# Hybrid SSM, pooling and attention layer: SSM groups every 7.5 steps, their memory handed to the output stage during the last projections, output weights requested earlier

## The chip, the cores and the metric

One core of a Trainium2 chip runs the whole layer in one launch. The metric is the device time of an execution in microseconds. The kernel before took 1631.17 us in the median of three runs (1629.35 to 1631.57).

## The reference

The input x has 4096 tokens of 1024 channels in fp32. One layer is computed:

```
h = RMSNorm_pre(x)
su, sg, pu, pg, q, k, v, ag = split(h @ w_in)            # widths 256 256 256 256 512 128 128 512
y_ssm  = GLU(GELU(S5(su) + D*su)) * silu(sg)             # 16 groups, 64 complex states, both directions
y_pool = scale * GroupLinear(mean pools(pu) - pu) * silu(pg)
y_attn = windowed attention(q, k, v) * silu(ag)          # +-128 tokens, 8 heads, 2 KV heads
out = x + RMSNorm_post(concat(y_ssm, y_pool, y_attn) @ w_out)
```

## The kernel before

The tokens are cut into NB = 8 blocks of 512 (TB), a block into four tiles of 128. The channels are cut into NK = 8 chunks of 128. Each product in the large matrices is made of three matmuls on operands split into a high and a low part (hi·hi, hi·lo, lo·hi), so that weights and activations are split by ScalarE (a copy, L173) and VectorE (a subtraction, L162), function `split`.

The order of the work is written out by hand. `Slots` (L84) holds a table from step number to actions. `e.at(n, f)` puts f into step n, `e.gen` runs a generator whose `yield n` is a pause of n steps, and `e.step()` emits the actions of the present step, in the order in which they were put there. The main loop emits six matmuls of 512 columns and then calls `e.step()`: a step is six matmuls of TensorE's order. Each engine, and SyncE, which issues nearly all DMAs, runs its instructions in the order in which they were emitted and waits for semaphores in that order.

The stages, by steps: projections of the first kind (0 to 191), query, key and value projections (192 to 383) with attention behind them, gate projections (384 to 575, `p3_block`: six chunks of four steps in each of eight blocks), and from 576 on the output stage (`w_out_k`: one step for one token tile and one chunk, eight steps for a tile).

Step 422 (48·NB + ATT_TAIL) calls `to_p3`. It opens the pools of the SSM stage and plans the 16 SSM groups, group g from step 422 + int(8·g) on, the last one at 542. A group's actions (list at L1080) are numbered from its start: load 0, angles 3 (GpSimd), their sines 5 to 7 (ScalarE), input products 9, direct product 10, `turn_re` 10 and `turn_im` 11 (VectorE, with a GpSimd sum in 11), `turn_sum` 12 (GpSimd), scans 13 and 14, `back_cos` 16 (VectorE), `back_sin` 17 and `back_sum` 20 and 21 (GpSimd), state products 24 and 25 (TensorE), copy 26, store 28. The SSM products are in fp32 and run as two instructions each. The tile wt of a group has two buffers.

The last gate block begins at step b0 = 552. In it each chunk n ends at step 552 + 4n + 3; one step later ScalarE evacuates its PSUM bank (two banks in turn, L1122), and three steps after that SyncE stores the gate (L1123). After each of these chunks `load_wo` asks for the two halves of output weight chunk 2 + n (256 KB each, three buffers "raw") and splits them four steps later, the subtraction another step later. The weights take the buffers that the projection weights of the chunk have released.

The first mixer tiles: pooling of block 0 (`y_pool`, two rounds of GpSimd sums, a ScalarE copy and VectorE operations) from step 546, attention tiles (`y_attn`) from 563 and 570. In the output stage 18 steps use chunks 2 to 7 of three token tiles. At the seventh of them, step 582, `to_c` finishes what is left of gates and SSM, closes the pools "gp" and "sv" of the SSM stage, opens the last stage's pools in their memory, and starts `y_ssm(0)` (its GLU products eight steps later), the loads of weight chunks 0 and 1, two residual tiles and the mixer tiles of block 1. The loop that follows (L1429) waits, by empty steps, until `YK[0, 0]` and `YK[0, 1]` of `y_ssm(0)` are there.

Of the kernel before, what the change touches and what calls it, by code (L numbers as in the profile page):

```python
# [10 lines left out]
F32 = mybir.dt.float32  # L11
F32R = mybir.dt.float32r
# [4 lines left out]
P = 128  # L17
SEQ = 4096
DM = 1024
# [53 lines left out]
    return c  # L73


SSM_PACE = 8.0
ATT_TAIL = 38
WARM = 8
P2_OPEN = 24 * NB + 15
# [50 lines left out]
def hybrid_kernel(ctx, tc, A, out):  # L130
# [56 lines left out]
    def split(hi, lo, src, eng, lag=1, scale=None):  # L187

        copy(hi, src)
        if lag:  # L190
            e.at(e.now + lag, lo_part, lo, src, hi, eng)
        else:
            lo_part(lo, src, hi, eng)
# [99 lines left out]
    def sched_x(b):  # L293
        b0 = 24 * b
        if b >= NB + RAWB:
            for i, d in enumerate((-12, -10, -4, -3)):
                e.at(b0 + d, x_load, b, i, label="main")
            return
        for i, (d, n_, sp_) in enumerate(((-22, -14, -13), (-20, -12, -11), (-18, -10, -4), (-16, -8, -3))):
            e.at(b0 + d, x_dma, b, i, label="main")  # L300
            if b == 1:
                e.at(b0 - 15 + 2 * i, x_sq, b, i, label="main")
                n_, sp_ = (-2, -2, -2, -1)[i], (-2, -2, -1, 0)[i]
            e.at(b0 + n_, x_norm, b, i, label="main")
            e.at(b0 + sp_, x_split, b, i, label="main")
# [648 lines left out]
    def p3_open():  # L954
        cw = ctx.enter_context(tc.tile_pool(name="cw", bufs=1))
        XTP[0] = ctx.enter_context(tc.tile_pool(name="xt3", bufs=3))
        ph = ExitStack()
        gp = ph.enter_context(tc.tile_pool(name="gp", bufs=3))
        sv = ph.enter_context(tc.tile_pool(name="sv", bufs=1))
        GP[0] = (gp, "g", "p3")  # L960
        rho = cw.tile([P, G], F32, name="rho")
        dma(out=rho, in_=rhod[:, :])
        psc = cw.tile([P, 2], F32, name="psc")
        dma(out=psc, in_=A["pool_scale"])
        gbc = cw.tile([P, DM], F32, name="gbc")
        dma(out=gbc, in_=A["post_g"])
        glb = cw.tile([P, 6], F32, name="glb")
        dma(out=glb[:, 0:4], in_=A["glu_b"])
        ts(glb[:, 4:6], glb[:, 2:4], 0.5, ALU.mult)
        gw = cw.tile([P, 2, 2, 4, P], F32R, name="gw")  # L970

        def glu_weights():
            for kk in range(2):
                raw = wraw.tile([P, 4, P], F32, tag="raw", name="raw")
                dma(out=raw.rearrange("p m c -> p (m c)"), in_=A["glu_w"][:, kk])
                yield 5
                split(gw[:, 0, kk], gw[:, 1, kk], raw, V)

        e.gen(e.now + 6, glu_weights(), label="main")

        gs = []
        for n in range(2):
            gt = sv.tile([P, 2, NC], F32, name=f"gs{n}")
            V.memset(gt[0:64, :, 0:1], 0.0)
            V.memset(gt[64:128, :, NC - 1:NC], 0.0)
            gs.append(gt)
        return dict(ph=ph, sv=sv, gs=gs, gbc=gbc, glb=glb, gw=gw, rho=rho, psc=psc)
# [99 lines left out]
    WO = {}  # L1087
    WO2 = [None]

    def load_wo(slot, kk, late=False):  # L1090
        def go(hf):
            if hf == 0:
                WO[kk] = (WO2[0] if late else wpool).tile([P, 2, DM], F32R, tag="w", name="wo")
            raw = wraw.tile([P, TB], F32, tag="raw", name="rawo")
            dma(out=raw, in_=A["w_out"][kk, :, hf * TB:(hf + 1) * TB])
            e.at(e.now + 4, prep, hf, raw)

        def prep(hf, raw):
            hs = slice(hf * TB, (hf + 1) * TB)
            split(WO[kk][:, 0, hs], WO[kk][:, 1, hs], raw, V)  # L1100
        e.at(slot, go, 0, label="main")
        e.at(slot + 1, go, 1, label="main")

    def p3_block(s):
        e.label = "p3"
        b = 2 * NB + s
        b0 = 24 * b
        if s < NB - 1:
            sched_x(b + 1)

        def ev_g(dst, c, o):
            def go():
                pool, tg, e.label = GP[0]
                g = pool.tile([P, TB], F32, tag=tg, name="gg", bufs=2 if tg == "tmp" else 3)
                if e.label == "p2":

                    h = pool.tile([P, TB], F32, tag=tg, name="gh", bufs=2)
                    S.activation(out=h, in_=o, func=AF.Copy, scale=0.5)
                    S.activation(out=g, in_=h, func=AF.Tanh)
                    e.at(e.now + 2, lambda: stt(g, g, 1.0, h, ALU.add, ALU.mult))  # L1120
                else:
                    S.activation(out=g, in_=o, func=AF.Silu)  # L1122
                e.at(e.now + 3, lambda: dma(out=dst[s, :, c, :], in_=g))  # L1123
            e.at(e.now + 1, go)

        for n, (m, dst, c) in enumerate([(CH_SG + c, sgate, c) for c in range(2)]
                                        + [(CH_AG + c, agate, c) for c in range(4)]):
            chunk(b, m, n % 2, lambda o, dst=dst, c=c: ev_g(dst, c, o), n == 0)
            if s == NB - 1:
                load_wo(e.now, 2 + n)  # L1130


    YK = {}
# [10 lines left out]
    def xt_tile(nm):  # L1144
        return XTP[0].tile([P, 2, HW], F32, tag="xt", name=nm)

    def y_pool(s, psc):

        en, pg, sc = xt_tile("en"), xt_tile("pgl"), xt_tile("psum")
        dma(out=en, in_=pud[:, :, s * TB:s * TB + HW])  # L1150
# [3 lines left out]
        for cc in range(2):  # L1154
# [21 lines left out]
                V.tensor_copy(out=x[:, 8 + c_.start:8 + c_.stop], in_=a[:, c_])  # L1176
            stt(pg[:, cc, 0:TB], x[:, 8:520], psc[:, cc:cc + 1], pg[:, cc, 0:TB], ALU.mult, ALU.mult)
            yield 1
        yk = ytile()
        split(yk[:, 0], yk[:, 1], pg[:, :, 0:TB], V)  # L1180
        yield 1
# [185 lines left out]
    for s in range(NB):  # L1367
        p2_block(s, R2)
    GP[0] = (R2["at"], "tmp", "p2")
    R3 = {}  # L1370

    def to_p3():
        e.settle("p2")
# [4 lines left out]

    e.at(48 * NB + ATT_TAIL, to_p3, label="main")
    b0 = 24 * (3 * NB - 1)  # L1380
    e.at(b0 - 6, lambda: e.gen(e.now, y_pool(0, R3["psc"])), label="main")
    e.gen(b0 + 11, y_attn(0, 0), label="main")
    e.gen(b0 + 18, y_attn(0, 1), label="main")
    for s in range(NB):
        p3_block(s)

    e.label = "main"
    KS = list(range(2, NK))

    R4 = {}  # L1390

    def to_c():
        e.settle("p3")
        e.settle("ssm")
        R3["ph"].close()
        R4.update(R3)
        XK2[0] = ctx.enter_context(tc.tile_pool(name="xk2", bufs=8 - XBUF))
        WO2[0] = ctx.enter_context(tc.tile_pool(name="w2", bufs=2))
        for n_, nm, bufs in (("ld", "ld4", 1), ("tp", "tp4", 2), ("xo", "xo4", 2), ("s4", "s4", 4)):
            R4[n_] = ctx.enter_context(tc.tile_pool(name=nm, bufs=bufs))  # L1400
        e.gen(e.now, y_ssm(0, R4))
        load_wo(e.now, 0, True)
        load_wo(e.now + 3, 1, True)
        for t in range(2):
            x_res(t, R4)
        e.gen(e.now + 1, y_pool(1, R4["psc"]))
        e.gen(e.now + 13, y_attn(1, 0))
        e.gen(e.now + 20, y_attn(1, 1))
        e.gen(e.now + 12, y_ssm(1, R4))


    early = [(j, kk) for ks in (KS[:4], KS[4:]) for j in range(2) for kk in ks] + [(2, kk) for kk in KS]
    for n_, (j, kk) in enumerate(early):
        if n_ == 6:
            to_c()
        w_out_k(0, j, kk, kk == 2, False)
        e.step()
    for s in range(NB):
# [74 lines left out]
```

## Time and profile before

| | before |
|---|---|
| median of the runs | 1631.17 us |
| the profiled execution | 1630.12 us, span 1628.3 us |
| TensorE busy | 1570.8 us, 96% |
| VectorE busy | 1064.6 us, 65% |
| ScalarE busy | 731.1 us, 45% |
| GpSimd busy | 620.4 us, 38% |
| mean granted TensorE clock | 0.989 |
| DMA | 267.56 MB, 164 GB/s over the span |

Busy time counts from an instruction's start to its modelled end; matmuls overlap in it. A wait in brackets or in the list of waits is idle time of an engine just before an instruction, with what ended it. In the profile PE is TensorE, DVE VectorE, ACT ScalarE, POOL GpSimd and SPq SyncE's DMA queue.

### The profile page before, as it was taken

The page shows a single profiled execution, that of the slowest core. Times are in us where ns is not written, and L with a number is a line of the kernel's source. Part 1 is how long each engine was busy: PE and PEld are TensorE (multiplying, and loading weights), DVE is VectorE, ACT ScalarE, POOL GpSimd, SP SyncE. Part 2 cuts the span into 40 slices and gives each one's busy share as a digit, 9 for nine tenths or more (in the row PEclk, how much of TensorE's full clock was granted, in tenths as well). Part 3 has the DMA queues.
Part 4 walks back from the last instruction along what each step waited for, and adds up shares of the span by engine and source line. Part 5 has one row for each costly group of instructions (what it writes and reads, how often), then busy time and mean ns, then how long its engine had stood idle before and what let it go on. Part 6 is the DMA issues. An engine that isn't in the chain of part 4 may idle for free.

```text
span 1628.3 us, 20646 instructions
## 1 busy us (share of the span) xinstructions
PE 1570.8 (96%) x7284; PEld 1273.6 (78%) x7284; DVE 1064.6 (65%) x1983; ACT 731.1 (45%) x1544; POOL 620.4 (38%) x366
## 2 busy tenths in 40 slices
PE   7999899999999999999999999999979999999998
PEld 6787678788888888888888867767757878888876
DVE  6774666436677777777987467777856656555451
ACT  5423334236666666666776543333233233332221
POOL 0321212102232333333233156666732645454642
PEclk9999999999999999999999999999999999999999
DMA  6598899871312112212224365555655564555442
GB/s 232 169 302 264 252 289 306 291 283 57 117 66 71 66 66 86 103 66 91 97 98 149 115 225 194 183 171 182 222 158 167 169 197 144 177 170 193 156 155 78
DMA packets 131691, 267.56 MB, mean 164 GB/s; under 512 B 32386, under 2 KB 65922, under 8 KB 119812
## 3 DMA queue, kind: packets, MB, share of 16 engines
q1 hardware_dynamic: 126020, 251.57, 47.4%
q10 hardware_dynamic: 5568, 14.68, 2.7%
q8 instruction: 57, 0.93, 0.2%
q14 instruction: 46, 0.38, 0.1%
HBM read 173.25 MB, written 94.01 MB: 164 GB/s over the span
## 4 chain that ended last, share of the span: by engine, by line
PE 67%; DMA 15%; DVE 8%; issue 4%; POOL 3%; ACT 2%; SPq 1%; ACTq 0%; POOLq 0%; DVEq 0%
PE mm L350 9%; PE mm L351 9%; PE mm L352 9%; DMA xs<-in_x_dram 7%; PE po L848 5%; PE mm L361 5%; PE tp L858 5%; PE o L1264 5%; PE o L1262 5%; PE o L1263 5%; PE s L819 3%; PE s L818 3%; PE y L1071 1%; POOL ot L162 1%; DMA rawo<-in_w_out_dram 1%
## 5 line engine op out<-in xcount | busy, mean ns | idle before, releaser
L350 PE MATMUL mm<-xk,w 128*128 128x512 f32 x968 | 400.6, 414 | 2.1 <-ACT xk L268 1.3
L352 PE MATMUL mm<-xk,w 128*128 128x512 f32 x968 | 379.8, 392 | 1.3 <-DVE w L162 1.3
L351 PE MATMUL mm<-xk,w 128*128 128x512 f32 x968 | 380.2, 393 | 0.0
L162 POOL TENSOR_TENSOR ns<-ns,es 128x1536 f32<-128x1536 f32 (+1 forms) x64 | 172.4, 2694 | 409.8 <-ACT pp L173 187.0
L350 PEld LDWEIGHTS mm<-xk,w 128*128 128x128 f32 x968 | 182.7, 189 | 44.7 <-issue 7.5
L352 PEld LDWEIGHTS mm<-xk,w 128*128 128x128 f32 x968 | 182.3, 188 | 42.0 <-DVE w L162 2.2
L351 PEld LDWEIGHTS mm<-xk,w 128*128 128x128 f32 x968 | 182.7, 189 | 40.5 <-issue 9.1
L1262 PE MATMUL o<-wo,yk 128*128 128x512 f32 x512 | 201.2, 393 | 6.5 <-ACT gg L1122 6.0
L1264 PE MATMUL o<-wo,yk 128*128 128x512 f32 x512 | 201.0, 393 | 2.1 <-DVE yk L165 2.1
L820 DVE CUSTOM_DVE_ANT_0 ns<-s,cst,nsink 128x384 f32<-128x384 f32 (+1 forms) x256 | 145.8, 607 | 84.6 <-PE s L819 83.4
L1263 PE MATMUL o<-wo,yk 128*128 128x512 f32 x512 | 200.4, 391 | 0.0
L173 ACT ACTIVATE pp<-tp 128x512 fp32r<-128x512 f32 x188 | 112.2, 597 | 170.2 <-PE tp L858 169.3
L361 PE MATMUL mm<-xk,w 128*128 128x512 f32 x552 | 152.1, 420 | 13.2 <-ACT xk L173 6.3
L809 ACT ACTIVATE ns<-ns,nm 128x384 f32<-128x384 f32 (+1 forms) x256 | 152.3, 598 | 2.0 <-DVE nm L820 2.0
L162 DVE TENSOR_TENSOR pp<-tp,pp 128x512 fp32r<-128x512 f32 x188 | 129.2, 688 | 18.8 <-ACT pp L173 17.4
L361 PEld LDWEIGHTS mm<-xk,w 128*128 128x128 f32 x552 | 104.7, 196 | 45.2 <-ACT xk L173 10.3
L848 PE MATMUL po<-pp,vr 128*128 128x512 f32 x376 | 127.8, 421 | 0.0
L162 POOL TENSOR_TENSOR xk<-xt,xk 128x512 fp32r<-128x512 f32 x32 | 54.3, 1704 | 178.3 <-ACT xk L173 140.4
L858 PEld LDWEIGHTS tp<-cst,ns 128*128 128x128 f32 x752 | 93.0, 140 | 34.6 <-issue 10.1
L858 PE MATMUL tp<-cst,ns 128*128 128x128 f32 x752 | 112.7, 272 | 7.3 <-DVE pp L162 7.3
L1262 PEld LDWEIGHTS o<-wo,yk 128*128 128x128 f32 x512 | 97.1, 190 | 27.9 <-ACT gg L1122 6.5
L1264 PEld LDWEIGHTS o<-wo,yk 128*128 128x128 f32 x512 | 96.9, 189 | 23.1 <-DVE yk L165 2.6
(269 smaller groups left out, 2569.6 us busy)
## 6 DMA issues: line engine op xcount, KB each, us to landing
xk<-xd SPq DMA_DIRECT2D x60, 1024.0 KB
xd<-xk SPq DMA_DIRECT2D x32, 1024.0 KB
xt<-in_xT_dram SPq DMA_DIRECT2D x35, 512.0 KB
xres<-in_x_dram SPq DMA_DIRECT2D x32, 512.0 KB
out_dram<-ot SPq DMA_DIRECT2D x31, 512.0 KB
xs<-in_x_dram ACTq DMA_DIRECT2D x24, 512.0 KB
raw<-in_w_in_dram SPq DMA_DIRECT2D x32, 256.0 KB
yattn<-ysb SPq DMA_DIRECT2D x32, 256.0 KB
```

Source lines behind the costliest of these rows:

```text
L162: return eng.tensor_tensor(out=out, in0=in0, in1=in1, op=op)
L350: T.matmul(o, lhsT=w[:, 0, k], rhs=xh, start=(k == 0), stop=False)
L351: T.matmul(o, lhsT=w[:, 0, k], rhs=xl, start=False, stop=False)
L352: T.matmul(o, lhsT=w[:, 1, k], rhs=xh, start=False, stop=(k == NK - 1))
L361: T.matmul(o, lhsT=w[:, i, k], rhs=XK[b, k][h], start=(n == 0), stop=(n == 3 * NK - 1))
L809: S.activation(out=ns[:, hh, :nk], in_=ns[:, hh, :nk], func=AF.Exp, scale=-1.0, bias=nm[:, hh:hh + 1], accum_out=su[:, hh:hh + 1])
L820: V.tensor_tensor_reduce(out=ns[:, hh, :nk], in0=sp_[:, :nk], in1=cst[:, C_D + c0:C_D + c0 + nk], scale=-(2.0 ** -(h + 1)), scalar=R["nsin ...
L848: T.matmul(po, lhsT=VR[:, (ta + kb) % 8, kv], rhs=pp[:, i], start=(kb == 0 and i == 0), stop=(kb == nkb - 1 and i == 1))
L858: T.transpose(tp[:, hh], ns[:, hh, kb * P:(kb + 1) * P], ident)
L1262: T.matmul(o, lhsT=y[:, 0, ts_], rhs=WO[kk][:, 0, hs], start=first, stop=False)
L1263: T.matmul(o, lhsT=y[:, 0, ts_], rhs=WO[kk][:, 1, hs], start=False, stop=False)
L1264: T.matmul(o, lhsT=y[:, 1, ts_], rhs=WO[kk][:, 0, hs], start=False, stop=last)
```

## The change

The groups' spacing goes from 8 to 7.5 steps: group g starts at 422 + int(7.5·g), group 12 at 512, 13 at 519, 14 at 527, the last at 534. Of the SSM stage's pools only "sv" is closed at the hand-over; "gp", which holds the gates, stays open and has two buffers instead of three. `y_pool(0)` starts at 522 and holds its result from being split until 558. `y_attn(0, 0)` starts at 561, `y_attn(0, 1)` at 569. The halves of output weights 2 to 7 are requested at 552 + 4n + 4 + 2·half - 5 and split at 552 + 4n + 4 + 2·half, copy and subtraction in the same step. `to_c` is put at step 567. It closes "sv", opens the last stage's pools in another order (the small ones "s4" with two buffers instead of four), loads output weights 0 and 1 as one transfer of 512 KB each into the residuals' buffers, splits them seven steps later, and starts `y_ssm(0)`. What it did for the residuals and block 1 is done by `to_d`, at the fourth step of the output stage, 579.

```diff
-SSM_PACE = 8.0
+SSM_PACE = 7.5
@@ p3_open
-        gp = ph.enter_context(tc.tile_pool(name="gp", bufs=3))
+        gp = ctx.enter_context(tc.tile_pool(name="gp", bufs=2))
@@ load_wo
-    def load_wo(slot, kk, late=False):
+    def load_wo(slot, kk):
+
+        raw = {}
+
         def go(hf):
+            raw[hf] = wraw.tile([P, TB], F32, tag="raw", name="rawo")
+            dma(out=raw[hf], in_=A["w_out"][kk, :, hf * TB:(hf + 1) * TB])
+
+        def prep(hf):
             if hf == 0:
-                WO[kk] = (WO2[0] if late else wpool).tile([P, 2, DM], F32R, tag="w", name="wo")
-            raw = wraw.tile([P, TB], F32, tag="raw", name="rawo")
-            dma(out=raw, in_=A["w_out"][kk, :, hf * TB:(hf + 1) * TB])
-            e.at(e.now + 4, prep, hf, raw)
-
-        def prep(hf, raw):
+                WO[kk] = wpool.tile([P, 2, DM], F32R, tag="w", name="wo")
             hs = slice(hf * TB, (hf + 1) * TB)
-            split(WO[kk][:, 0, hs], WO[kk][:, 1, hs], raw, V)
-        e.at(slot, go, 0, label="main")
-        e.at(slot + 1, go, 1, label="main")
+            split(WO[kk][:, 0, hs], WO[kk][:, 1, hs], raw[hf], V, 0)
+
+        for hf in range(2):
+            e.at(slot + 2 * hf - 5, go, hf, label="main")
+            e.at(slot + 2 * hf, prep, hf, label="main")
+
+    def load_wo_late(kk, pool):
+        raw = pool.tile([P, DM], F32, tag="xres", name="rawl")
+        dma(out=raw, in_=A["w_out"][kk])
+        yield 7
+        WO[kk] = WO2[0].tile([P, 2, DM], F32R, tag="w", name="wo")
+        split(WO[kk][:, 0], WO[kk][:, 1], raw, V)
@@ p3_block
+        if s == NB - 2:
+            for n in range(6):
+                load_wo(b0 + 24 + 4 * n + 4, 2 + n)
...
-            if s == NB - 1:
-                load_wo(e.now, 2 + n)
@@ y_pool, ahead of the split of its result
+        if hold > e.now:
+            yield hold - e.now
@@ the main order
-    e.at(b0 - 6, lambda: e.gen(e.now, y_pool(0, R3["psc"])), label="main")
-    e.gen(b0 + 11, y_attn(0, 0), label="main")
-    e.gen(b0 + 18, y_attn(0, 1), label="main")
...
+    e.at(b0 - 30, lambda: e.gen(e.now, y_pool(0, R3["psc"], b0 + 6)), label="main")
+    e.gen(b0 + 9, y_attn(0, 0), label="main")
+    e.gen(b0 + 17, y_attn(0, 1), label="main")
     def to_c():
-        e.settle("p3")
         e.settle("ssm")
         R3["ph"].close()
         R4.update(R3)
+        for n_, nm, bufs in (("ld", "ld4", 1), ("tp", "tp4", 2)):
+            R4[n_] = ctx.enter_context(tc.tile_pool(name=nm, bufs=bufs))
+        WO2[0] = ctx.enter_context(tc.tile_pool(name="w2", bufs=2))
         XK2[0] = ctx.enter_context(tc.tile_pool(name="xk2", bufs=8 - XBUF))
-        WO2[0] = ctx.enter_context(tc.tile_pool(name="w2", bufs=2))
-        for n_, nm, bufs in (("ld", "ld4", 1), ("tp", "tp4", 2), ("xo", "xo4", 2), ("s4", "s4", 4)):
+        for n_, nm, bufs in (("xo", "xo4", 2), ("s4", "s4", 2)):
             R4[n_] = ctx.enter_context(tc.tile_pool(name=nm, bufs=bufs))
+        for kk in range(2):
+            e.gen(e.now, load_wo_late(kk, R4["xo"]))
         e.gen(e.now, y_ssm(0, R4))
-        load_wo(e.now, 0, True)
-        load_wo(e.now + 3, 1, True)
+
+    e.at(48 * NB + ATT_TAIL + 2 + int(SSM_PACE * (G - 1)) + 31, to_c, label="main")
...
+    def to_d():
         for t in range(2):
             x_res(t, R4)
         e.gen(e.now + 1, y_pool(1, R4["psc"]))
...
-        if n_ == 6:
-            to_c()
+        if n_ == 3:
+            to_d()
```

## Rows read from the trace of the kernel before

**Rows 1.** TensorE's waits, 900 to 1280 us: total, times, longest, in us.
```profile
PE o L1262 <- ACT gg L1122: 6.0, 1, 6.0
PE y L1071 <- POOL wt L162: 2.6, 1, 2.6
PE o L1264 <- DVE yk L165: 2.1, 1, 2.1
```

**Rows 2.** Time line of TensorE: start, length in us; in brackets the idle time before.
```profile
1186.14 1.12 PE L1071 MATMUL y<-wt,rec 128*128 128x512 f32 x2 [2.64 <-POOL wt L162]
...
1218.15 0.79 PE L1262 MATMUL o<-wo,yk 128*128 128x512 f32 x1 [6.05 <-ACT gg L1122]
...
1222.49 0.39 PE L1263 MATMUL o<-wo,yk 128*128 128x512 f32 x1
...
1256.69 0.80 PE L1264 MATMUL o<-wo,yk 128*128 128x512 f32 x1 [2.12 <-DVE yk L165]
...
1259.84 0.43 PE L1262 MATMUL o<-wo,yk 128*128 128x512 f32 x1
```

**Rows 3.** Windows: length, busy by engine (us), granted clock, DMA share, GB/s.
```profile
1186.00:1194.00 8.00, 7.86 (x33) 6.17 (x34) 7.86 (x7) 2.04 (x4) 5.48 (x4) 1.00 0.00 0
...
1218.00:1226.00 8.00, 7.85 (x26) 6.32 (x27) 2.77 (x4) 1.77 (x4) 0.00 (x0) 0.73 0.89 251
```

**Rows 4.** Time line of SyncE's queue.
```profile
1178.26 16.24 SPq L1095 DMA_DIRECT2D rawo<-in_w_out_dram  x2
...
1218.50 0.96 SPq L1271 DMA_DIRECT2D xres<-in_x_dram  x2
```

**Rows 5.** Time line of ScalarE.
```profile
1216.04 0.63 ACT L173 ACTIVATE wo<-rawo 128x512 fp32r<-128x512 f32 x1 [5.99 <-DMA rawo<-in_w_out_dram]
...
1228.38 1.06 ACT L1209 ACTIVATE q<-ys 128x1024 f32<-128x1024 f32 x1 [6.99 <-DMA ys<-ybuf]
```

**Rows 6.** The chain that ended last, in the SSM stage: start, us, what.
```profile
1127.25 4.11 PE mm L361 x18
...
1137.69 0.86 PE y L1071 x2
...
1152.95 0.86 PE y L1071 x2
```

**Rows 7.** Time line of VectorE.
```profile
1124.29 0.69 DVE L162 TENSOR_TENSOR wt<-vr,cs 128x512 f32<-128x512 f32 x1 [2.29 <-PE vr L1032]
...
1134.95 1.22 DVE L1056 TENSOR_TENSOR_SCAN gs<-rho,wt 64x511 f32<-64x511 f32 x1
1136.20 1.23 DVE L162 TENSOR_TENSOR wt<-gs,cs 128x1024 f32<-128x1024 f32 x1
...
1172.64 0.34 DVE L162 TENSOR_TENSOR psum<-psum,cst 128x8 f32<-128x8 f32 x1
...
1235.18 2.06 DVE L165 SCALAR_TENSOR_TENSOR yr<-q,yr 128x1024 fp32r<-128x1024 f32 x1
```

**Rows 8.** Time line of GpSimd.
```profile
1137.58 2.35 POOL L162 TENSOR_TENSOR gs<-gs,cs 128x1024 f32<-128x1024 f32 x1 [3.71 <-DVE wt L162]
...
1142.31 1.04 POOL L162 TENSOR_TENSOR ang<-rec 128x512 f32<-128x512 f32 x1
...
1147.66 1.29 POOL L162 TENSOR_TENSOR wt<-wt,gs 128x512 f32<-128x512 f32 x1
...
1152.66 2.36 POOL L162 TENSOR_TENSOR gs<-gs,cs 128x1024 f32<-128x1024 f32 x1 [3.71 <-DVE wt L162]
...
1172.91 1.30 POOL L162 TENSOR_TENSOR wt<-wt,gs 128x512 f32<-128x512 f32 x1
...
1176.36 1.57 POOL L162 TENSOR_TENSOR psum<-en 128x527 f32<-128x527 f32 x1 [0.90 <-DVE en L1176]
1178.00 5.94 POOL L162 TENSOR_TENSOR psum<-psum 128x525 f32<-128x525 f32 x3
1184.02 2.06 POOL L162 TENSOR_TENSOR wt<-wt,gs 128x512 f32<-128x512 f32 x1
```

More of the change, by code (lines that the diff above doesn't have):

```diff
@@ L1113, in go @@
                 pool, tg, e.label = GP[0]
-                g = pool.tile([P, TB], F32, tag=tg, name="gg", bufs=2 if tg == "tmp" else 3)
+                g = pool.tile([P, TB], F32, tag=tg, name="gg", bufs=2)
                 if e.label == "p2":
@@ L1145, in xt_tile, with y_pool @@
         return XTP[0].tile([P, 2, HW], F32, tag="xt", name=nm)
-    def y_pool(s, psc):
+    def y_pool(s, psc, hold=0):
         en, pg, sc = xt_tile("en"), xt_tile("pgl"), xt_tile("psum")
@@ L1369, in hybrid_kernel @@
     GP[0] = (R2["at"], "tmp", "p2")
-    R3 = {}
+    R3, R4 = {}, {}
     def to_p3():
@@ L1380, in hybrid_kernel, with to_c @@
     b0 = 24 * (3 * NB - 1)
-    e.at(b0 - 6, lambda: e.gen(e.now, y_pool(0, R3["psc"])), label="main")
-    e.gen(b0 + 11, y_attn(0, 0), label="main")
-    e.gen(b0 + 18, y_attn(0, 1), label="main")
+    e.at(b0 - 30, lambda: e.gen(e.now, y_pool(0, R3["psc"], b0 + 6)), label="main")
+    e.gen(b0 + 9, y_attn(0, 0), label="main")
+    e.gen(b0 + 17, y_attn(0, 1), label="main")
+    def to_c():
+        e.settle("ssm")
+        R3["ph"].close()
+        R4.update(R3)
+        for n_, nm, bufs in (("ld", "ld4", 1), ("tp", "tp4", 2)):
+            R4[n_] = ctx.enter_context(tc.tile_pool(name=nm, bufs=bufs))
+        WO2[0] = ctx.enter_context(tc.tile_pool(name="w2", bufs=2))
+        XK2[0] = ctx.enter_context(tc.tile_pool(name="xk2", bufs=8 - XBUF))
+        for n_, nm, bufs in (("xo", "xo4", 2), ("s4", "s4", 2)):
+            R4[n_] = ctx.enter_context(tc.tile_pool(name=nm, bufs=bufs))
+        for kk in range(2):
+            e.gen(e.now, load_wo_late(kk, R4["xo"]))
+        e.gen(e.now, y_ssm(0, R4))
+    e.at(48 * NB + ATT_TAIL + 2 + int(SSM_PACE * (G - 1)) + 31, to_c, label="main")
     for s in range(NB):
@@ L1388, in hybrid_kernel @@
     KS = list(range(2, NK))
-    R4 = {}
-    def to_c():
-        e.settle("p3")
[L1394 to L1397, printed above, removed]
-        WO2[0] = ctx.enter_context(tc.tile_pool(name="w2", bufs=2))
-        for n_, nm, bufs in (("ld", "ld4", 1), ("tp", "tp4", 2), ("xo", "xo4", 2), ("s4", "s4", 4)):
-            R4[n_] = ctx.enter_context(tc.tile_pool(name=nm, bufs=bufs))
-        e.gen(e.now, y_ssm(0, R4))
-        load_wo(e.now, 0, True)
-        load_wo(e.now + 3, 1, True)
+    def to_d():
         for t in range(2):
```

## The prediction

> **What bounds the kernel now.** I read the busy shares first, then the list of what TensorE waited for, then the time lines of the stretches in which it waited. The reader sees TensorE at work for nearly the whole span, and from the start of the SSM stage on its long waits lie in one place, the passage from the projections to the output stage: 6.05 us for a gate's evacuation by ScalarE and 2.12 us for a mixer tile, and just before it 2.64 us for an SSM sum on GpSimd [rows 1, 2]. So a change is worth what it takes from these waits, less what it adds on the queues that feed TensorE.
>
> The long wait is one chain. SyncE's issues of the last gate stage's weight halves took 16.24 us, with nothing moved meanwhile (0 GB/s) [rows 3, 4]: they wait for a raw buffer that VectorE frees late, behind SSM and pool work. Much later ScalarE idles 5.99 us for such a half [rows 5], and the gate evacuation that frees the PSUM bank stands behind it in ScalarE's order. After the wait the granted clock was 0.73 in that stretch [rows 3], that is, between the two levels of 1.2 and 2.4 GHz: ten matmuls from 1218.15 to 1222.49 take 4.34 us where ten of 0.228 us (4.11/18 [rows 6]) would take 2.28, so 2.06 us more. After the 2.12 us wait seven take 3.15 us (1256.69 to 1259.84) instead of 1.60: 1.55 us more. The 2.64 us wait was followed by a clock of 1.00 [rows 3].
>
> **The change part by part.** A step is six matmuls: 1.37 us. One SSM group adds five fp32 products of 0.86 us each [rows 6]: 4.30 us. Eight steps with one group are then 15.26 us, just the spacing of the rows (1137.69 to 1152.95); 7.5 steps are 14.57.
>
> Pace: TensorE's work stays the same, so directly 0. What it squeezes is the loop through a group: the two buffers of wt are reused by the group two later, whose first turn (step 10 of its own) now falls on the very step 25 in which the older group's second state product reads them; at a pace of 8 it fell one step behind. From the first turn to the end of the second sum is 1124.29 to 1148.95, 24.7 us [rows 7, 8]; two groups take 29.1, less 0.86 for the product: 28.3. Slack 3.6 us, so I take 0; if the loop grows by more, SSM sets the pace (third rival).
>
> Pool work of tile 0: same instructions, started 24 steps earlier (522 instead of 546) and held until 558 for its split. The end of SSM loses its 2.64 us wait; the work now lies among groups 12 and 13. The order that results on GpSimd: back_sin of 12 (529), turn_im of 13 and angles of 14 (530), then the second pool block (530), and only then turn_sum of 13 (531) and the sums of 12 (532, 533). TensorE needs the first sum at step 536. Count from turn_re of 13 (529), which waits for group 11's product in that step. VectorE: two turns of 0.69, then pool's edge work; from its first edge operation to GpSimd's second block is 1172.64 to 1176.36, 3.72 us. Together 5.1. The block: 1176.36 to 1183.94, 7.58. Then turn_sum and sum at 1.30 alone, 2.06 beside VectorE [rows 7, 8]: 2.6 to 4.1. Sum 15.3 to 16.8. TensorE meanwhile has the direct product and seven steps, 0.86 + 9.59 = 10.45. Its wait is 4.9 to 6.4; I take 5.6, without a fall of the clock, as after the 2.64. Bounds: 2.6 (the wait of before merely moves) and 8.5 (6.4 and a fall of 2.06). ScalarE's pool copy (534) waits for the block too; behind it stands the gate evacuation of 537, whose bank is not due before 540.
>
> Output weights 2 to 7: twelve halves as before, asked for five steps before their split instead of four, the split's two operations in one step instead of two. The first split is at 556, when SSM's last VectorE work (550) is out of the way. Queued behind a waiting half are, on SyncE, gate stores and attention loads, on ScalarE the evacuations; with 6.8 us of lead the loads are hidden; a late half costs nothing until the evacuation behind it is three steps (4.1 us) late, when its bank is due. This takes away the 6.05 + 2.06.
>
> Hand-over: at 567, not 582, three steps after the last store (562); so the SSM memory is free but for that store, and the second-stage tile's inputs start earlier. The 2.12 + 1.55 disappears: those tiles are due at 594. But the GLU products now stand at the end of 575, inside the projections, again eight steps after the hand-over. Before, from the hand-over's first transfer (1218.50) to VectorE's last operand (1237.24) were 18.7 us [rows 4, 7], ScalarE getting the SSM tile at 1228.38 [rows 5]; 1 MB went ahead of it (residuals), as now 1 MB does (weights 0 and 1). TensorE came later still, because it had been standing. Now SyncE reaches the hand-over after weight half 7, which waits for half 4's split, and that for the tile that projection 2 releases at the start of 564: some 2.0 us later (copy, subtraction, issue). The products are due 12 steps after 564, 16.4 us. 2.0 + 18.7 - 16.4 = 4.3 us late. Bounds: 0 (the early issue finds shorter queues) and 6.4 (SyncE only at its own step 567, 4.1 us). I take 4.3 and a clock loss of 1.5, that of the 2.12 wait, the nearest in size; bounds 0 and 2.06. The gate evacuation of 576 stands behind the second attention tile's copy (575) on ScalarE, which waits for transfers queued behind the same 2 MB: even if the GLU operands come early, some 2 us would be waited for there.
>
> Weights 0 and 1 as one transfer each rather than two: as many bytes and columns, split on ScalarE and VectorE, due at 594: 0 either way. Gate buffers 2 instead of 3: a store has five steps (6.8 us) to land, 0; small buffers 2 instead of 4, residuals and pool tile 1 three steps earlier: their work is due 15 steps later, 0; each could cost or give 0.5.
>
> Sum: removed 2.64 + 8.11 + 3.67 = 14.4; added 5.6 + 4.3 + 1.5 = 11.4; net -3.0. The profiled execution took 1630.12 (span 1628.3), 1.05 under the median of 1631.17: 1627.1 there, 1628.2 as a median.
>
> **The rivals.** *The hand-over costs nothing.* For it: the idle transfers beside the 16.24 us [rows 3, 4] are filled, so queues ahead of 567 may be short. Against: the hand-over asks for 2 MB at once and the attention tiles for 1 MB on each side of it. Net -14.4 + 5.6 = -8.8: 1622.4; with the pool wait at its lower bound 1619.
>
> *The passage only changes its wait.* Late GLU operands at the upper bounds, 6.4 + 2.06, and 5.6: 14.1 against 14.4. 1631, no change. For it: ScalarE's order above. Against: less is queued there than before.
>
> *SSM becomes the bound: slower.* A GpSimd sum of 1.30 us alone took 2.06 with VectorE at work, so the two exclude each other for part of the time. Per group GpSimd has 2.35 + 1.04 + 4 x 1.30 = 8.6 us, and VectorE four scans of 1.22 and a product of 1.23, 6.1 [rows 7, 8]. If all exclude each other the sum is 14.7, below 15.26 but above 14.57, and it lies in series with a gap while the next turn is not there: from back_sin to back_sin is 15.1 us (1137.58 to 1152.66). If 15.1 is a floor, 15 spacings lose 0.5 each, 8 us, on top of the forecast: 1636. It decides when the loop passes 28.3 us. For it: this sum. Against: part of the 15.1 is waiting for TensorE, and the rows of the pair overlap by some 0.15 us an operation.
>
> The Trainium skill, page "SBUF — State Buffer", section "Who interferes with whom", has a rule for this: VectorE operations with two SBUF inputs and GpSimd operations lock a shared port pair for a whole instruction. By that rule the pair would be the floor as in this rival, 1636; with no lock the forecast stands. The trace agrees on the lock, with 2.06 against 1.30.
>
> **How the numbers follow.** Forecast 0.40, hand-over free 0.27, changed wait 0.15, SSM bound 0.18. About 0.2% (3.3 us) is what a measurement can tell from no change: faster means under 1627.9. Faster: 0.27 and 0.19 of the forecast, 0.46; within: 0.21 and 0.12, 0.33; slower: 0.18 and 0.03, 0.21. The range, from the rival with both lower bounds to the slower one: 1618 to 1637; the forecast's own is 1624 to 1632.
>
> **What would show it.** Right: no wait of TensorE for the last gate evacuation over 2 us; one of some 5 us at an SSM state product in the last projection block but one, on a GpSimd sum; some 4 us at the first GLU products, on VectorE. Wrong: state products waiting in group after group (third rival), no wait at the GLU products (first), or a state product that isn't held up by the pool work.

## The result, and the profile after

The changed kernel takes 1642.47 us (median of 8 runs, 1639.62 to 1647.29), the kernel before beside it 1633.37 (8 runs): ratio 1.0056, 95% interval 1.0039 to 1.0073. It is slower by some 9 us (6.4 to 11.9); the forecast was 1628.2, in a range of 1618 to 1637.

Where the difference lies is first a question of place. One transfer marks the end of the second stage (step 422), the load of rho. Its row in the time line of SyncE, kernel before, whose span is 1628.3 us:

```profile
928.57 0.59 SPq L962 DMA_DIRECT2D rho<-rhod  x1
```

The same row of the changed kernel, whose span is 1638.7 us:

```profile
933.23 0.60 SPq L962 DMA_DIRECT2D rho<-rhod  x1
```

From there to the end are 699.7 us before and 705.5 after: 5.8 more. A second profile of the kernel before (run e0) has it at 931.68 of 1630.5, thus 698.8 to the end. e0 was run to see whether the changed kernel is slower ahead of that row by something constant. The same kernel came there 3.1 us later than in its first profile, so at least that much is spread between executions or chips. Up to that row the two kernels issue the same instructions, and yet that part took 927 to 939 us in the profiles of this study, 928.57 and 931.68 in two of one kernel. I call what follows it *the tail* and compare tails; the 4.7 us ahead of it can't be put down to the change by one profile of each. The list of TensorE's waits, changed kernel, 900 to 1300 us (total, times, longest):

```profile
PE z L990 <- ACT yr L1234: 6.4, 1, 6.4
PE y L1071 <- POOL wt L162: 4.2, 1, 4.2
PE mm L361 <- DMA xk<-xd: 2.7, 3, 1.8
PE o L1276 <- DVE ot L165: 2.3, 1, 2.3
PE z L991 <- DVE yr L165: 1.6, 1, 1.6
PE vr L1032 <- issue: 1.2, 1, 1.2
```

None of the three waits of before [rows 1] is here under its old name except the state product's, and that is longer and at another group. What follows each wait is seen in TensorE's time line:

```profile
1153.76 1.42 PE L1071 MATMUL y<-wt,rec 128*128 128x512 f32 x2 [4.16 <-POOL wt L162]
...
1228.58 0.79 PE L990 MATMUL z<-yr,gw 128*128 128x512 f32 x1 [6.44 <-ACT yr L1234]
1230.96 0.80 PE L991 MATMUL z<-yr,gw 128*128 128x512 f32 x1 [1.59 <-DVE yr L165]
...
1236.24 0.46 PE L1277 MATMUL o<-wo,yk 128*128 128x512 f32 x1
...
1274.09 0.80 PE L1276 MATMUL o<-wo,yk 128*128 128x512 f32 x1 [2.32 <-DVE ot L165]
...
1277.24 0.44 PE L1277 MATMUL o<-wo,yk 128*128 128x512 f32 x1
```

And in windows (length, busy by engine, granted clock, DMA share, GB/s):

```profile
1152.00:1160.00 8.00, 6.25 (x14) 3.20 (x15) 7.40 (x5) 0.00 (x0) 5.58 (x4) 0.79 0.00 0
1224.00:1232.00 8.00, 1.83 (x4) 1.14 (x5) 5.67 (x6) 5.67 (x9) 1.75 (x1) 0.63 0.27 83
1272.00:1280.00 8.00, 5.91 (x19) 4.75 (x20) 2.66 (x5) 1.12 (x5) 3.07 (x3) 0.79 0.31 99
```

Each is followed by half clock (1.2 of 2.4 GHz: a product every 0.43 us instead of 0.23). The state product: 4.16 and 0.21 of 8 us, 1.7, together 5.9. The GLU products: 6.44 and 1.59; the first product takes 0.79 where 0.23 is usual, and twelve take 5.28 us (1230.96 to 1236.24) instead of 2.74, so 3.1 of clock; together 11.1. The output tile: 2.32, and seven products in 3.15 instead of 1.60; together 3.9. These are 20.9 us against the 14.4 of before. With the small waits (2.7 and 1.2 here; 0.9, 0.5, 0.3 and 0.2 before, and 1.9 at GLU products after 1280 us, which the changed kernel no longer has) it is 24.8 against 18.2: 6.6 more, where the tails differ by 5.8.

The pool block, in GpSimd's time line:

```profile
1144.37 1.57 POOL L162 TENSOR_TENSOR psum<-en 128x527 f32<-128x527 f32 x1 [0.90 <-DVE en L1188]
1146.01 5.13 POOL L162 TENSOR_TENSOR psum<-psum 128x525 f32<-128x525 f32 x3
1151.22 1.26 POOL L162 TENSOR_TENSOR wt<-wt,t 128x512 f32<-128x512 f32 x1
1152.44 3.40 POOL L162 TENSOR_TENSOR wt<-wt,gs 128x512 f32<-128x512 f32 x2
```

It stands where the prediction had put it, ahead of the turn and the sums, and takes 6.8 us. The hand-over, in SyncE's:

```profile
1209.10 0.92 SPq L1110 DMA_DIRECT2D rawl<-in_w_out_dram  x2
1210.12 1.90 SPq L1216 DMA_DIRECT2D ys<-ybuf  x2
1212.06 4.36 SPq L1219 DMA_DIRECT2D sg<-sgate  x1
...
1217.68 3.88 SPq L1096 DMA_DIRECT2D rawo<-in_w_out_dram  x2
```

in ScalarE's:

```profile
1218.87 1.06 ACT L1223 ACTIVATE q<-ys 128x1024 f32<-128x1024 f32 x1 [6.46 <-DMA ys<-ybuf]
...
1224.56 0.58 ACT L1136 ACTIVATE gg<-mm 128x512 f32<-128x512 f32 x1
1227.47 1.06 ACT L1234 ACTIVATE yr<-q 128x1024 fp32r<-128x1024 f32 x1 [2.33 <-DVE q L165]
...
1232.32 0.58 ACT L1136 ACTIVATE gg<-mm 128x512 f32<-128x512 f32 x1
```

and in VectorE's:

```profile
1221.81 1.23 DVE L162 TENSOR_TENSOR q<-q,ys 128x1024 f32<-128x1024 f32 x1
1224.68 1.62 DVE L162 TENSOR_TENSOR wo<-rawo,wo 128x512 fp32r<-128x512 f32 x1 [1.64 <-ACT wo L173]
1226.22 1.21 DVE L165 SCALAR_TENSOR_TENSOR q<-q,ys 128x1024 f32<-128x1024 f32 x1
1229.08 0.69 DVE L162 TENSOR_TENSOR wo<-rawo,wo 128x512 fp32r<-128x512 f32 x1 [1.65 <-ACT wo L173]
1229.69 1.22 DVE L165 SCALAR_TENSOR_TENSOR yr<-q,yr 128x1024 fp32r<-128x1024 f32 x1
```

From the first transfer to ScalarE's square are 9.8 us, as before (1218.50 to 1228.38, 9.9 [rows 4, 5]). From there to VectorE's end of yr are 12.0 us (1218.87 to 1230.91), before 8.9 (1228.38 to 1237.24 [rows 5, 7]). The three engines' orders show why: a subtraction of a weight half stands on VectorE ahead of each step of the chain and waits 1.64 us for ScalarE's part of that half, which on ScalarE stands behind the chain's own step before (the tanh, then yr). The gate evacuations of 1224.56 and 1232.32 are late with it.

### The profile page after: what moved, and what is told of

Its sections match the earlier page's. It is cut to its first block, busy times and chain, and to the rows that moved or that the text cites. A ratio compares the mean times of both kernels' runs of the same rounds, so it can differ in the third digit from the quotient of the medians.

```text
span 1638.7 us, 20664 instructions
## 1 busy us (share of the span) xinstructions
PE 1574.6 (96%) x7284; PEld 1275.6 (78%) x7284; DVE 1066.1 (65%) x1981; ACT 732.5 (45%) x1542; POOL 620.2 (38%) x366
## 4 chain that ended last, share of the span: by engine, by line
PE 77%; DMA 10%; DVE 7%; issue 2%; POOL 1%; SPq 1%; ACT 1%; ACTq 0%; POOLq 0%; DVEq 0%
PE mm L350 9%; PE mm L351 9%; PE mm L352 9%; PE o L1276 7%; PE o L1278 7%; PE o L1277 7%; PE po L848 5%; PE mm L361 5%; PE tp L858 5%; DMA xs<-in_x_dram 3%; PE s L819 3%; PE s L818 3%; PE y L1071 2%; DMA xk<-xd 1%; DMA xd<-xk 1%
```

## The experiments

All times are medians beside the kernel before on the same chip; the tail is that of the one profiled execution (in e3 and e4 this was the longest of the six). Two tails of the kernel before differ by 0.9 us, so differences of a microsecond or two between tails say little.

| run | us | ratio to before (95%) | tail |
|---|---|---|---|
| the changed kernel | 1642.5 | 1.0056 (1.0039 to 1.0073) | 705.5 |
| e1 | 1641.1 | 1.005 (1.0034 to 1.0066) | 707.1 |
| e2 | 1644.9 | 1.0064 (1.0046 to 1.0081) | 701.7 |
| e3 | 1646.4 | 1.008 (1.0065 to 1.0095) | 712.8 |
| e4 | 1645.6 | 1.0073 (1.005 to 1.0095) | 715.6 |
| e5 | 1639.8 | 1.0031 (1.0016 to 1.0046) | 701.6 |
| e6 | 1643.7 | 1.0048 (1.0032 to 1.0063) | 707.5 |
| e8, pace alone | 1630.5 | 0.9979 (0.9959 to 0.9998) | 693.8 |
| e9 | 1631.4 | 0.9977 (0.9961 to 0.9993) | 696.6 |
| e10 | 1635.6 | 1.0002 (0.9984 to 1.0019) | 697.6 |
| e11 | 1635.8 | 1.0006 (0.999 to 1.0023) | 698.4 |
| e12 | 1631.3 | 0.9982 (0.9968 to 0.9995) | 696.0 |
| e13 | 1625.3 | 0.9947 (0.9928 to 0.9967) | 689.9 |
| e14 | 1627.0 | 0.9948 (0.9933 to 0.9962) | 692.2 |
| e15 | 1625.2 | 0.9944 (0.9929 to 0.9959) | 689.5 |
| e16 (on a chip where before takes 1625.3) | 1624.6 | 0.9993 (0.9981 to 1.0006) | 698.1 |

**Taking away one wait of the changed kernel at a time (e1 to e4).** e1 puts the GLU products eight steps later:

```diff
-        yield 3 if s else 1
+        yield 3 if s else 9
```

> The changed kernel with one edit: the GLU products of the first SSM tile stand eight steps later, at 583 instead of 575; they are still done (587 and 591) before they are due at 594. Theory A (the waits that the new places make are the loss, each of its own): the two waits at the GLU products, 6.44 and 1.59 us, and the 3.2 us of half clock behind them go, 11 us in all, and the other waits stay: some 1631 where the changed kernel takes 1642. Theory B (ScalarE and the transfers bound the passage, the GLU products only show it): the wait moves to the evacuation of the last gate chunk or to an output weight, and no more than 4 us are gained. Theory C (the loss lies in the SSM pace of 7.5): 0 to 3 us are gained.

The GLU waits went, and TensorE's list shows in their place:

```profile
PE o L1276 <- ACT gg L1136: 9.1, 2, 5.6
```

Two gate evacuations (1223.49 and 1230.74) stand behind the square of the SSM tile on ScalarE, which waits 6.93 us for its transfer. So the late instruction is not the loss by itself; everything behind it in ScalarE's order is late too.

e2 starts the pool work of tile 0 after most of the sums:

```diff
-    e.at(b0 - 30, lambda: e.gen(e.now, y_pool(0, R3["psc"], b0 + 6)), label="main")
+    e.at(b0 - 5, lambda: e.gen(e.now, y_pool(0, R3["psc"], 0)), label="main")
```

> The changed kernel with one edit: the pool tile of block 0 starts at step 547 instead of 522 and is split without being held, so that its second GpSimd block (555) stands behind the last SSM sums. Theory A: the 4.16 us wait of a state product for a GpSimd sum and the 1.9 us of half clock behind it go, 6 us, the rest stays: some 1636 against 1642. Theory B: the same at this place, but SyncE waits for the pool tile's buffers before the attention tile's loads (561), so that the hand-over comes later and the GLU products wait 1 to 3 us longer: 3 to 5 us gained. Theory C: with the pace at 7.5 the sums are late without pool work too: state products wait 2 us or more still.

The state product's 4.16 went (0.29 us is left, at an early group, 975.78), and this grew:

```profile
PE z L990 <- ACT yr L1234: 11.5, 1, 11.5
```

SyncE's issue of two weight halves now lasted 4.94 us (1204.90), waiting for a raw buffer, and the hand-over began at 1210.42, later against the products. In the tail 3.8 us are gained, in the median nothing.

e3 puts residuals and tile 1's work back to where they were:

```diff
-        if n_ == 3:
+        if n_ == 6:
```

> The changed kernel with one edit: the residuals and mixer tiles of block 1 start at step 582 instead of 579, as in the kernel before. Theory A: the 2.32 us wait for the first finished output tile (its bank is freed by VectorE, which had a split of block 1 before it) falls to the 0.46 us of the kernel before and the half clock behind it goes, 3 to 4 us: some 1638.5 against 1642. Theory B (the small buffers, two instead of four, hold up the first output tiles): the wait stays at 2 us or more, and nothing is gained.

It is no help: the output tile's wait stays at 2.35, a wait of 4.5 for tile 1's GLU operand appears, and the tail grows by 7.3. So moving block 1 back does not take this wait away. Nor are the two small buffers needed for it: e13 below has four of them and waits 2.25 at that place. The move to three steps earlier is worth keeping, if the early hand-over is. e4 has the three edits together:

> The changed kernel with the edits of the other three together. Theory A: the waits are separate and their prices add up: 11 + 6 + 3.5 = 20 us less than the changed kernel, some 1622, and 10 us less than the kernel before. Theory B (one queue behind them all): the gain is that of the largest, some 1631.

Gate evacuations are waited for 14.9 us in all. The prices of the waits do not add up.

**What holds the passage (e5, e6, e11, e10).** e5 lets the SSM tile's loads begin at 567 as in the changed kernel, but its work only at 577, so that the gate evacuations no longer stand behind it on ScalarE:

```diff
-        yield 3 if s else 2
+        yield 3 if s else 10
```

> The changed kernel with one edit: the loads of the first SSM tile stay at step 567, but its whole chain (ScalarE's square first) starts eight steps later, at 577 instead of 569; GLU products at 583. With the GLU products alone moved, the wait went to the evacuations of the last gate chunks, 3.52 and 5.60 us, which stand in ScalarE's order behind that square while it waits 6.9 us for its transfer. Theory B1 (this place in ScalarE's order is the cause): the evacuations come when their chunk is done, no wait of TensorE over 2.5 us at the first output matmuls (what the second attention tile's copy at 575 may hold up), gain 7 to 11 us: 1632 to 1635 where the changed kernel takes 1642. Theory B2 (the transfers bound the passage, whatever the order): 5 us or more are waited for at the evacuations, an output weight or an attention tile, gain under 4.

5.4 us for the last gate evacuation remain, now because the weight half ahead of it on ScalarE comes late, in ScalarE's time line

```profile
1223.68 0.63 ACT L173 ACTIVATE wo<-rawo 128x512 fp32r<-128x512 f32 x1 [5.88 <-DMA rawo<-in_w_out_dram]
```

It was asked for at 1217.00, behind the hand-over's and the attention tile's transfers. e6 also starts the pool tile at step 430, among the first groups:

```diff
-    e.at(b0 - 30, lambda: e.gen(e.now, y_pool(0, R3["psc"], b0 + 6)), label="main")
+    e.at(48 * NB + ATT_TAIL + 8, lambda: e.gen(e.now, y_pool(0, R3["psc"], b0 + 6)), label="main")
```

> The edit of the run before this, and the pool tile of block 0 started at step 430, among the first SSM groups, held until 558 as in the changed kernel. Theory B1 and the pool's price of its own: the 4.16 us wait and 1.9 us of half clock go as well, since no more than one group's sums stand behind the pool block; 5 to 6 us under the run before this, some 1628. Rival: what the earlier end of the projections gains is waited for in the passage again, as when the pool tile was moved to 547: within 2 us of the run before this.

A miss: the pool block holds up the first groups' sums by 7.5 us instead. Neither start among the groups had room for it: 4.16 us of wait from 522, 7.5 from 430.

e11 is e5 with the loads of weights 0 and 1 ten steps after the hand-over:

```diff
-            e.gen(e.now, load_wo_late(kk, R4["xo"]))
+            e.gen(e.now + 10, load_wo_late(kk, R4["xo"]))
```

> The changed kernel with the SSM tile's work from step 577 (as in the run with the tile's work late) and the loads of output weights 0 and 1 (1 MB) begun ten steps after the hand-over instead of with it. Theory T, the megabyte ahead in the transfer queues makes the last gate weight's half late: ScalarE's wait for that half falls from 5.88 to under 2.5 us, TensorE's wait for the evacuation from 5.44 to under 2; 1634 to 1637 us. Theory U, it is requested late, since its raw buffer comes free late: the request stays near 1217 us, and the wait stays over 4.5; 1639 to 1641 us.

ScalarE waited 3.58 us for the half instead of 5.88, TensorE 2.6 instead of 5.4, and the ratio fell from 1.0031 to 1.0006. The half is the first of the two that SyncE asks for in these rows, e5 and e11:

```profile
1217.00 0.89 SPq L1096 DMA_DIRECT2D rawo<-in_w_out_dram  x2
...
1217.23 1.17 SPq L1096 DMA_DIRECT2D rawo<-in_w_out_dram  x2
```

and in e11 ScalarE takes it at

```profile
1224.76 0.63 ACT L173 ACTIVATE wo<-rawo 128x512 fp32r<-128x512 f32 x1 [3.58 <-DMA rawo<-in_w_out_dram]
```

Less than the first theory asked, and in another way. From the request to ScalarE's copy are 6.7 us in e5 and 7.5 in e11, so the half did not land faster after its request for having no megabyte ahead of it. It was asked for earlier: counted from the row of rho (933.80 and 937.59) at 283.2 in e5 and 279.6 in e11. Between the first issue of the hand-over and this request SyncE spends 8.0 us in e5 (from 1209.04) and 4.8 in e11 (from 1212.48). So the megabyte's place ahead on SyncE is worth a good part of this wait. Whether the issues behind it (3.37 us for the gate tile in e5, 2.15 in e11) are longer for its bytes in the queues stays open. Besides, the copies of weights 0 and 1 (1.99 us on ScalarE, between the half and the evacuation) moved behind the evacuation too. The intervals of the two ratios overlap a little (1.0016 to 1.0046, 0.999 to 1.0023), so the gain in time is less sure than that of the wait.

e10 leaves the early hand-over out altogether and keeps pace, weight loads and pool place (built up from the kernel before, with its gate and small buffers, on e9 below; the lines that come on top):

```diff
+    e.at(b0 - 30, lambda: e.gen(e.now, y_pool(0, R3["psc"], b0 + 6)), label="main")
+    e.gen(b0 + 9, y_attn(0, 0), label="main")
+    e.gen(b0 + 17, y_attn(0, 1), label="main")
```

> As the run with pace and gate weights, and also tile 0's pool and attention work where the changed kernel has it (pool 24 steps earlier, held; attention 2 and 1 steps earlier). The hand-over stays late, at step 582, so this is the changed kernel without its early hand-over (and with three gate buffers and four small ones). Theory A, the early hand-over is what costs the passage: no wait at GLU products before step 594, only the state product's 4 us with its half clock of some 2; 1630 to 1635 us. Theory B, the pool work is what costs: about the changed kernel's 1640 to 1643 us.

Its list of waits:

```profile
PE y L1071 <- POOL wt L162: 4.2, 1, 4.2
PE mm L361 <- DMA xk<-xd: 2.6, 3, 1.9
PE o L1284 <- DVE yk L165: 2.1, 1, 2.1
PE o L1282 <- ACT gg L1142: 0.5, 1, 0.5
```

The gate evacuation is waited for 0.5 us, the GLU products not at all. Between this and the changed kernel lie 0.54%, 8.8 us (5 to 13 by the two intervals; the tails differ by 7.9): that is what the early hand-over (with the moves and buffers that come with it) costs.

**What the other parts are worth (e8, e9).** e8 is the kernel before with one number changed:

```diff
-SSM_PACE = 8.0
+SSM_PACE = 7.5
```

> The kernel before with the pace alone at 7.5. Theory A (the pace costs nothing by itself): state products wait only for the pool tile's blocks, 2 to 5 us in all; the rest as before, so 1630 to 1638 where the kernel before takes 1634. Theory C (at 7.5 VectorE and GpSimd are the bound): state products wait in most groups, 0.5 us or more for each, 1641 or more.

Its waits:

```profile
PE o L1262 <- ACT gg L1122: 2.7, 1, 2.7
PE o L1264 <- DVE yk L165: 2.1, 1, 2.1
PE mm L361 <- DMA xk<-xd: 2.1, 3, 1.6
```

No state product is waited for in any group. The 2.64 of before stood at group 14's second product, whose sum lay behind the pool block; now both sums of that group come before the pool work. The last group's second sum still stands behind the block, and is just in time: it ends at 1195.94 (1194.65 and 1.29), and the product starts at 1196.00. The gate's 6.05 is 2.7: the issue that lasted 16.24 us [rows 4] lasts 8.41 (1190.95), since VectorE gets through SSM and pool work sooner. Faster by 0.2%, with a tail 5 to 6 us shorter.

This refutes the third rival's floor of 15.1 us: at a period of 14.57 it would have cost some 8 us, and no state product waits. It does not show that VectorE and GpSimd ran beside each other freely. The sum of all their operations, 14.7 us, is 0.13 more than the period, 2 us over 15 spacings, and the loop's slack was 3.6. The Trainium skill (page "SBUF — State Buffer", section "Who interferes with whom") calls the shared port pair an exclusive lock. The rows agree that operations lengthen beside each other [rows 8]; how full the lock is, e8 can't tell.

e9 adds only the earlier requests of weights 2 to 7 (the new form of load_wo, planned in the last gate block but one):

```diff
+        if s == NB - 2:
+            for n in range(6):
+                load_gate(b0 + 24 + 4 * n + 4, 2 + n)
-            if s == NB - 1:
-                load_wo(e.now, 2 + n)
```

> The kernel before with two parts of the change alone: groups every 7.5 steps, and output weights 2 to 7 requested five steps before their split at planned places of the last gate block (weights 0 and 1, the pool tile and the hand-over stay as before). With the pace alone the profile showed waits of 2.73 (the last gate evacuation, followed by half clock), 2.12 (mixer tile) and 0.43. Theory A, the weight loads do what the prediction said: the 2.73 goes with its half clock, about 4 us less than with the pace alone, 1626 to 1628 us, ratio 0.995 to 0.997 against before. Theory B, in the passage a removed wait is replaced by the next one in ScalarE's and the tiles' order: 2.73 goes but the mixer tile's wait grows by as much, 1629 to 1632.

The wait grew to 3.54. The halves' places are early, but ScalarE still waits for transfers (5.0 and 4.5 us), with the pool work at the end of SSM ahead of them on VectorE and three raw buffers all in use: the half of the 5.0 was asked for at 1200.05, when VectorE had just freed a buffer (1200.03). Neither theory: the part alone gives nothing; in e10, with the pool work out of the way (and attention earlier), the wait was gone.

**A passage without its first wait (e12, e13).** e12 is e9 with more room:

```diff
-    wraw = ctx.enter_context(tc.tile_pool(name="wraw", bufs=3))
+    wraw = ctx.enter_context(tc.tile_pool(name="wraw", bufs=4))
-            e.at(slot + 2 * hf - 5, go, hf, label="main")
+            e.at(slot + 2 * hf - 7, go, hf, label="main")
-            x_res(t, R4)
+            e.at(e.now + 1, x_res, t, R4)
```

(and two gate buffers instead of three).

> The run with pace and gate weights, and: a fourth raw buffer for weight halves (paid for by the third gate buffer), output weights 2 to 7 requested seven steps before their split instead of five, and the residuals' loads asked for one step later, so that the SSM tile's loads go ahead of them. With three buffers ScalarE waited 5.0 and 4.5 us for such halves and TensorE 3.54 for the gate evacuation behind the second. Theory A, the number of raw buffers sets when a half is requested, and the passage has no other limit as near: the 3.54 goes with its half clock of some 2, the mixer tile's 2.12 falls under 1 as its loads lead; 1624 to 1627 us, ratio 0.993 to 0.996. Theory B, a removed wait is replaced by the next, as at the output tiles: the 3.54 goes, but the mixer tile or the output bank is waited for 2 to 4 us; 1628 to 1632 us, ratio 0.996 to 0.999.

3.27 us at the same place, but the half was in time; now ScalarE stood at the second attention tile's copy, whose product on GpSimd waited for its load:

```profile
1221.54 2.36 POOL L162 TENSOR_TENSOR ya<-ya,ga 128x1024 f32<-128x1024 f32 x1 [8.83 <-DMA ga<-agate]
```

e13 begins the attention tiles two steps earlier:

```diff
-    e.gen(b0 + 11, y_attn(0, 0), label="main")
-    e.gen(b0 + 18, y_attn(0, 1), label="main")
+    e.gen(b0 + 9, y_attn(0, 0), label="main")
+    e.gen(b0 + 16, y_attn(0, 1), label="main")
```

> The run with four raw buffers, and the two attention tiles of tile 0 begun two steps earlier (9 and 16 steps into the last gate block instead of 11 and 18). Theory A, the last gate evacuation is late only because the second attention tile's copy ahead of it in ScalarE's order waits for GpSimd's product, whose loads were asked for late: the 3.27 us falls under 0.7 and no half clock follows at step 576; 4 to 5 us less than with four raw buffers, 1625 to 1628 us, ratio 0.994 to 0.997 against before. Theory B, another operand comes late in its place (a weight half behind the earlier loads): 2 us or more are still waited for at step 576; ratio 0.997 to 0.999.

Its waits:

```profile
PE mm L361 <- DMA xk<-xd: 2.7, 3, 1.7
PE o L1280 <- DVE ot L165: 2.3, 1, 2.3
PE o L1282 <- DVE yk L165: 2.1, 1, 2.1
PE o L1280 <- ACT gg L1142: 0.5, 1, 0.5
```

The first theory, and the version that beats both kernels: 1625.27 us, 0.53% under the kernel before, with the pace, the early weights, a free raw buffer and earlier attention tiles, but without the early hand-over and the early pool work.

**The wait behind the mixer tile (e14 to e16).** e14 moves tile 0's GLU products two steps earlier (`if n_ == 4` for `if n_ == 6` at the late hand-over):

> The run with attention earlier, and the late hand-over two steps earlier (580 instead of 582), which moves on TensorE alone the GLU products of tile 0; the other engines keep their order. The mixer tile (2.12 us and 1.5 of half clock) is due when it was. Theory A, that wait is worth what it shows: it goes, the bank is waited for under 1 us as before, 3 to 3.7 us less than with attention earlier. Theory B, the bank of output tile 0 is next in line: it is waited for 2 to 2.7 us with its half clock, and the time falls by under 1 us.

The mixer tile's 2.12 fell to 0.91; the bank of output tile 0 was waited for 1.89, and half clock came behind it. No gain in the ratio, much as theory B had it. e15 plans the bank's last reading a step earlier:

```diff
-        yield 0 if last else 2
+        yield 0 if last else 1 if t < 3 else 2
```

> The run with the GLU products two steps earlier, and for output tiles 0 to 2 the last reading of the bank planned one step after the statistics instead of two. Theory B (the bank is the next wait): its wait falls by 0.8 to 1.4 us, and if it falls under 1 us the half clock goes too; 1 to 3 us less than with the GLU products two steps earlier alone. Theory A (there is no bank wait over 1 us to remove): no change within 0.5 us in the stretch.

1.84, no change: the plan did not hold the reading. In the profile a statistic on GpSimd holds it, behind tile 1's attention product:

```profile
1254.93 2.39 POOL L162 TENSOR_TENSOR ya<-ya,ga 128x1024 f32<-128x1024 f32 x1 [13.68 <-DMA ga<-agate]
1257.27 0.56 POOL L162 TENSOR_TENSOR rs<-ms,cst 128x1 f32<-128x1 f32 x1
```

e16 puts that product behind (`e.gen(e.now + 16, y_attn(1, 0))` for `+ 13`):

> The run with the bank free a step earlier, and tile 1's first attention tile begun three steps later, which puts its 2.39 us product on GpSimd behind the statistics of output tiles 0 and 1 instead of ahead of them. Theory G, GpSimd's order holds the bank: the statistic runs 2 us earlier, VectorE's reading of the bank follows, the bank wait falls from 1.84 under 0.5 us; 2 to 3 us less than with the bank free a step earlier, ratio 0.992 to 0.994 against before. Theory H, the chain itself is too long (squares, statistics, two readings), or VectorE's own order holds the reading (tile 1's SSM operand now stands ahead of it): the wait stays over 1.2 us and the ratio near 0.9944.

Its waits:

```profile
PE z L990 <- DVE yy L165: 7.4, 1, 7.4
...
PE o L1282 <- DVE yk L165: 0.9, 1, 0.9
...
PE o L1280 <- DVE ot L165: 0.2, 1, 0.2
```

GpSimd's order did hold the bank: 0.2 is left. But ScalarE then waited until 1263.01 for an output buffer whose store was late,

```profile
1263.01 0.60 ACT L1295 ACTIVATE ot<-o 128x512 f32<-128x512 f32 x1 [12.45 <-DMA out_dram<-ot]
```

and GLU products of tile 1 waited 7.4 us behind it. The store (1257.33) stood on SyncE behind an attention load (1256.92) that had waited 9.2 us for the very product that e16 put later. One cause shown, and a longer wait in its place: the tail is 8.6 us longer than e15's.

## Why the prediction was wrong

Two terms of the sum failed. The GLU products were put at 5.8 us (4.3 and 1.5) and cost 11.1, because the compute chain behind the transfers took 12.0 us instead of the 8.9 that were taken over from the old order, and began later. And the bank of the next output tile, due just behind the mixer tile, was put at nothing and cost 3.9. These are 9.2 of the 9.5 us between the forecast's -3.0 and the +6.5 of the waits. All three signs that were to show the forecast right did come (no gate evacuation, 4.16 at a state product, the GLU products waiting, though longer): they told the places of the waits, not their prices, and none looked at the bank.

*Bound and place of the waits.* Right: TensorE's waits at the end of SSM and in the passage make the difference, and a change is worth what it does there.

*Pace at 0, third rival.* The rival (SSM bound, 1636) was wrong in mechanism, although its time and sign came nearest; e8 shows no wait per group. The pace at 0 was mis-sized in the other direction: by itself it takes 5 to 6 us from the tail, because the end of SSM comes earlier against the pool work and the gate weights. The prediction counted these waits as removed by other parts, so this does not add to the error of the sum.

*Pool work, +5.6.* Right in mechanism and place: 4.16 of wait inside the bounds (the block took 6.8 us, not 7.58), and 1.7 of clock that I had left to the upper bound, 5.9 in all. But it was not the only way to lose the 2.64: with the pace alone that was gone already.

*Gate wait, -8.11.* It went, as the sum had it, but it could not be counted as gained apart from the GLU products. It is gained by the loads without the early hand-over (0.5 us left in e10). In the whole change the wait moves to the GLU products and, once these are put later, back to gate evacuations (9.1 in e1, 5.4 in e5): ScalarE's order, and what stands on SyncE ahead of the halves, hold both. The rival "the passage only changes its wait" named ScalarE's order, and got 0.15.

*GLU products, +4.3 and 1.5.* Mis-sized: 8.0 (6.44 and 1.59) and 3.1, beyond my upper bounds of 6.4 and 2.06. Transfers took what they took before (9.8 us against 9.9). The compute chain behind them took 12.0 instead of 8.9: I had taken the old chain's length over, though between other neighbours in the two engines' orders each weight half made its steps wait for one another. The start was later by the rest: the first transfer came 13.0 us ahead of the due time (1209.10 to 1222.14, the start of the wait) instead of 14.4. (The last store, 562, is five steps ahead of the hand-over, not three as the prediction has it; no term used that.)

*Mixer tile, -3.67.* Failed: it went, and 3.87 came at the next bank. Before, the mixer's wait and its half clock had covered that bank: 2.12 + 1.55 + 0.46 = 4.1 before; 2.12 + 2.25 = 4.4 in e13, where no half clock came between; 0.91 + 1.89 in e14 and a fall of the clock. Only e16 freed the bank, and there the holder was GpSimd's order. In the changed kernel the bank's reading (1273.30 on VectorE) had its statistic at 1270.80 and stood behind two operations of tile 1 (1270.76 and 1271.90); in e3, which moves these, behind a statistic of 2.05 us on VectorE (1271.27), beside tile 1's product on GpSimd. That VectorE's order held it in the changed kernel is read from the profile, not tested.

*Moves at 0.* Residuals and tile 1 earlier took away 1.9 us of GLU waits after 1280 us, and e3's miss agrees. The buffers I did not test by themselves.

By the measured terms the forecast's net -3.0 becomes 20.9 - 14.4 = +6.5, and the tails say +5.8 to +6.7. The median's 9.1 (6.4 to 11.9) is not in conflict with that; whether the part ahead of the tail adds some of it stays open.

## What to carry to other kernels

Before a wait is counted as gained, look for the next operand, bank or queue place due just behind it: here a mixer tile's 3.7 us covered a bank's, and a passage had three operands late one behind the other, with ScalarE's square, a weight half and an attention tile each ahead of a gate evacuation; only with the last of them in time did the gain come (e13). Work that is put earlier into an engine that runs in order must be costed with what stands between its steps there, not with the chain's old length, and an instruction that waits for a DMA holds everything behind it. Time the smallest part of a change alone: here one number gave a gain that the rest threw away.

## What the runs showed of the hardware

A wait's length did not tell whether half clock follows: after 2.12 us it did in the kernel before [rows 2] and not in e13, where the granted clock stayed at 1.00 over the whole stretch; after 2.64 it did not [rows 3], after 1.84 in e15 it did (0.79 from 1256 to 1264). The e13 window with the 2.12:

```profile
1250.00:1258.00 8.00, 4.16 (x18) 2.92 (x16) 5.70 (x9) 4.59 (x10) 3.20 (x3) 1.00 0.63 212
```

What sets it I can't say from these rows. And the first 930 us, same instructions in both kernels, differ by 3 us between two executions of one kernel (928.57 and 931.68), as much as the forecast's whole gain (3.0); parts of a change are better compared by tails and by many runs.
